# A second stage in three passes, its up projection by Strassen's seven products: decoder trunk on one Trainium2 core

## The chip, the cores and the metric

One core of a Trainium2 chip runs the whole kernel. The metric is the device time of one execution in microseconds. Engines go by the profile's names: PE multiplies matrices (PEld is its weight load), DVE, ACT and POOL work element by element, SP issues DMAs. PSUM has eight banks of 128 x 512 float32, in which PE leaves its sums.

## The reference

One layer of a decoder trunk, for 2048 prompt tokens and 32 sample tokens (8 sequences of 4) that share all weights, in float32:

```python
h = rms_norm(x, w_norm1) * (1 + sc1) + sh1
mix, ... = hybrid_mixer(h, ...)
x = x + gt1 * mix
h = rms_norm(x, w_norm2) * (1 + sc2) + sh2
x = x + gt2 * (jnp.square(jax.nn.relu(h @ w_up)) @ w_down)
y = rms_norm(x, w_norm_f)
```

The last step of the mixer is `concatenate([o_dn, o_gla]) @ w_o`. D is 1024; w_o is 1024 x 1024, w_up 1024 x 4096, w_down 4096 x 1024. The modulations sh, sc and gt come from a conditioning vector, one for the prompt and one for each sample sequence.

## The kernel before

Everything is kept transposed: features on the 128 partitions, tokens along the free dimension. There are 2080 tokens, the 32 samples first, in four groups (`TG`: 544, 512, 512, 512). Where a block is wider than PSUM's 512 it is cut (`BLK`: group 0 in two blocks of 272 columns, the others in one of 512). A float32 operand is split in two float32r parts, `hi` (a rounded copy) and `lo` (the rest), and `prod` (L239) makes a product of three matmuls for each 128 rows of the sum: hi x hi, hi x lo, lo x hi.

The first stage (`group`, L1132) goes group by group through the input projection and the two recurrences. It leaves the gated heads' two factors in DRAM (`oscr`, `zscr`).

The second stage (from L1230) runs in two halves, of groups 0 and 1, then 2 and 3. Each half has, for its two groups:

- `prep_o` (L1108): eight steps, each loads 128 rows of `oscr` and `zscr` on POOL's queue into `xo` and `zo` (two buffers each), multiplies them on DVE and splits the result (ACT the hi, DVE the lo).
- `out_proj` (L1253): eight products of 8 x 3 matmuls per block, `gated_add` (L1241) adds them to x on DVE, `sq_add` sums the squares.
- `norm2` (L1270): `sq_end` and `rsqrt` make the inverse root of the mean, then h is scaled, shifted and split into `hb` tiles.
- eight chunks (`ch`) of 512 hidden features: `up` (L1289) four times, with ReLU and Square on ACT and a split into the tiles `a` or `x`; then `down` (L1302) for eight output rows, with the sum over the chunks kept in SBUF by `gated_add`.
- `last_norm` (L1309) and the stores of y.

Weights come through `parts` (L205) and the six buffers `wb`. The first time, a weight of 128 x 1024 is loaded, ACT makes the hi (L225), another engine the lo (L226: DVE for the input projection, POOL for w_o, w_up and w_down), and both are stored in DRAM (`kept`, L201). Every later time both are loaded from there (L217). All weight DMAs are issued by SP in one order.

A tile framework lays the instructions out: it takes them in the order of the Python code, weighs what could run first, and writes for each engine a fixed sequence. An engine takes its own strictly in order. A tile's buffers go round; a new tile waits for the last reader of its buffer. Functions put into `late` are emitted at the next `flush()`.

## Time and profile before

| | us |
|---|---|
| median of 3 runs (lowest, highest) | 2911.71 (2907.19, 2912.94) |
| the profiled execution: its own time | 2916.36 |
| its span, first to last instruction | 2914.5 |
| PE busy / DVE busy / ACT busy / POOL busy | 2830.3 / 1488.0 / 889.3 / 265.6 |
| granted TensorE clock, mean | 0.987 |

The profile is one execution; its time lies 4.65 us above the median of the runs. Busy times are sums over the span. Matmuls overlap in the record: one of 512 columns is listed with some 0.40 us, and the next starts 0.23 us later, so rates are read from starts. The second stage's first matmul is at some 1212 us, its last at 2896.

### The profile page before, as it was taken

The numbers are of one execution on the slowest core, as the hardware profiler recorded it, in microseconds if no ns is written. First come the engines' busy times: TensorE is split into PE (matmuls) and PEld (weight loads), VectorE is DVE, ScalarE is ACT, GpSimd is POOL, SyncE is SP. The second block draws the span as 40 slices with busy tenths as digits, with TensorE's granted clock in tenths as the row PEclk, the third lists the DMA queues.
The fourth block names the chain that finished last, engine by engine and source line by source line (L and its number), as shares of the span: only waits on it lengthen the run. The fifth ranks groups of instructions, "written<-read, shape, count | busy, mean of one in ns | idle before, by whom it ended". The sixth has DMA issues, their size and how long they took to land.

```text
span 2914.5 us, 43962 instructions
## 1 busy us (share of the span) xinstructions
PE 2830.3 (97%) x17311; PEld 2395.6 (82%) x17311; DVE 1488.0 (51%) x3564; ACT 889.3 (31%) x2238; POOL 265.6 (9%) x204
## 2 busy tenths in 40 slices
PE   7999999999999999999999999999899999999997
PEld 5889977887778778888999999998788888888886
DVE  5997778666766776565233333334744222222225
ACT  3655534343444444323211221123222110011112
POOL 0100000000000100222221121122100000000000
PEclk9999999999999999999999999999999999999998
DMA  7565545456546445676333334334864222222224
GB/s 272 191 204 199 197 141 178 134 194 223 175 154 211 158 169 167 216 276 229 131 144 138 131 138 144 131 133 168 292 240 144 102 87 102 88 100 91 97 96 150
DMA packets 174272, 476.08 MB, mean 163 GB/s; under 512 B 36961, under 2 KB 50657, under 8 KB 173297
## 3 DMA queue, kind: packets, MB, share of 16 engines
q1 hardware_dynamic: 167520, 451.88, 44.5%
q0 software_dynamic: 6544, 21.38, 2.3%
q8 instruction: 137, 2.24, 0.3%
q14 instruction: 71, 0.57, 0.1%
HBM read 331.68 MB, written 141.79 MB: 162 GB/s over the span
## 4 chain that ended last, share of the span: by engine, by line
PE 81%; DVE 8%; DMA 5%; issue 3%; ACT 2%; POOL 1%; SPq 0%; DVEq 0%; POOLq 0%; ACTq 0%
PE gps L244 12%; PE gps L245 12%; PE gps L243 12%; PE cps L244 10%; PE cps L245 10%; PE cps L243 10%; PE gps L419 1%; PE mps L419 1%; DMA wb<-w_in 1%; DVE cv L837 1%; PE mps L1020 1%; DMA xo<-oscr 1%; PE mps L630 1%; PE cps L164 1%; DVE Um L915 1%
## 5 line engine op out<-in xcount | busy, mean ns | idle before, releaser
L243 PE MATMUL gps<-hb,wb 128*128 128x512 f32 (+1 forms) x1752 | 632.4, 361 | 5.9 <-ACT gkq L585 2.9
L245 PE MATMUL gps<-hb,wb 128*128 128x512 f32 (+1 forms) x1752 | 626.5, 358 | 2.4 <-POOL wb L226 1.7
L244 PE MATMUL gps<-hb,wb 128*128 128x512 f32 (+1 forms) x1752 | 627.3, 358 | 0.0
L243 PEld LDWEIGHTS gps<-hb,wb 128*128 128x128 f32 x1752 | 332.5, 190 | 59.5 <-issue 7.1
L245 PEld LDWEIGHTS gps<-hb,wb 128*128 128x128 f32 x1752 | 332.1, 190 | 45.8 <-POOL wb L226 1.9
L244 PEld LDWEIGHTS gps<-hb,wb 128*128 128x128 f32 x1752 | 332.3, 190 | 44.7 <-issue 2.7
L245 PE MATMUL cps<-hb,wb 128*128 128x512 f32 (+1 forms) x968 | 343.8, 355 | 4.8 <-POOL wb L226 4.8
L243 PE MATMUL cps<-hb,wb 128*128 128x512 f32 (+1 forms) x968 | 343.3, 355 | 4.9 <-DVE gas L1248 4.9
L244 PE MATMUL cps<-hb,wb 128*128 128x512 f32 (+1 forms) x968 | 343.8, 355 | 0.0
L226 POOL TENSOR_TENSOR wb<-wb 128x1024 fp32r<-128x1024 f32 x72 | 172.5, 2395 | 741.8 <-PE gps L244 408.6
L243 PEld LDWEIGHTS cps<-hb,wb 128*128 128x128 f32 x968 | 183.6, 190 | 32.1 <-issue 5.3
L245 PEld LDWEIGHTS cps<-hb,wb 128*128 128x128 f32 x968 | 183.6, 190 | 31.6 <-POOL wb L226 5.4
L244 PEld LDWEIGHTS cps<-hb,wb 128*128 128x128 f32 x968 | 183.5, 190 | 26.4 <-issue 0.2
L1296 ACT ACTIVATE e<-cps 128x512 f32<-128x512 f32 (+1 forms) x96 | 50.1, 522 | 499.2 <-PE cps L245 499.2
L225 ACT CAST wb<-wb 128x1024 fp32r<-128x1024 f32 (+1 forms) x104 | 109.3, 1051 | 295.2 <-DMA wb<-w_up 159.7
L1299 DVE CAST a<-e 128x272 fp32r<-128x272 f32 (+1 forms) x96 | 58.7, 613 | 251.9 <-ACT e L1297 251.8
L1299 DVE CAST x<-e 128x512 fp32r<-128x512 f32 x64 | 27.3, 427 | 277.6 <-ACT e L1297 277.6
L243 PE MATMUL cps<-a,wb 128*128 128x272 f32 (+1 forms) x460 | 149.5, 325 | 5.1 <-DVE gas L1248 3.7
L244 PE MATMUL cps<-a,wb 128*128 128x272 f32 (+1 forms) x460 | 149.4, 325 | 0.0
L245 PE MATMUL cps<-a,wb 128*128 128x272 f32 (+1 forms) x460 | 148.8, 324 | 0.0
L1296 ACT ACTIVATE e<-gps 128x512 f32<-128x512 f32 (+1 forms) x64 | 32.9, 514 | 341.7 <-PE gps L245 340.6
L1244 DVE SCALAR_TENSOR_TENSOR a<-cps,modT,a 128x512 f32<-128x512 f32 (+1 forms) x81 | 58.1, 717 | 134.5 <-PE cps L245 134.4
(472 smaller groups left out, 5199.6 us busy)
## 6 DMA issues: line engine op xcount, KB each, us to landing
wb<-k_w_in SPq DMA_DIRECT2D x168, 512.0 KB, 4.3
wb<-k_w_up SPq DMA_DIRECT2D x80, 512.0 KB, 4.2
wb<-k_w_down SPq DMA_DIRECT2D x80, 512.0 KB, 4.2
k_w_up<-wb SPq DMA_DIRECT2D x64, 512.0 KB, 2.8
k_w_down<-wb SPq DMA_DIRECT2D x64, 512.0 KB, 2.7
k_w_in<-wb SPq DMA_DIRECT2D x56, 512.0 KB, 3.4
wb<-k_w_o SPq DMA_DIRECT2D x48, 512.0 KB, 4.7
wb<-w_up SPq DMA_DIRECT2D x32, 512.0 KB, 3.6
```

Of the source, the lines that this page charges most:

```text
L164: T.matmul(ps[32 * j:32 * j + 32, :], lhsT=cs[:, 4 * hf + j, :], rhs=wt[hf][:, j, :], start=(hf == 0), stop=(hf == 1))
L225: S.copy(out=hi, in_=raw[:, 0:n])
L226: (V if name in ("w_in", "w_ts0", "w_ts1") else G).tensor_tensor(out=lo, in0=raw[:, 0:n], in1=hi.bitcast(F32), op=SUB)
L243: T.matmul(ps, lhsT=w[0][:, kw], rhs=x[0](kx), start=(i == 0), stop=False)
L244: T.matmul(ps, lhsT=w[0][:, kw], rhs=x[1](kx), start=False, stop=False)
L245: T.matmul(ps, lhsT=w[1][:, kw], rhs=x[0](kx), start=False, stop=(i == n - 1))
L419: T.matmul(ps, lhsT=h[hh][:, 4 * q + kk, c0:c0 + P], rhs=w[:, kk, :], start=(kk == 0 and i == 0), stop=(kk == 3 and i == 2))
L630: T.matmul(pa[0:i0, n, i0:i0 + 32], lhsT=ko[:, n, o:o + I, :], rhs=Q3[:, n, i0:i0 + 32], start=True, stop=True)
L837: V.scalar_tensor_tensor(out=cp, in0=raw[:, i:i + 512], scalar=wconv[:, ct, i:i + 1], in1=cp, op0=MUL, op1=ADD)
L1244: V.scalar_tensor_tensor(out=out[:, lo:c1], in0=ps[:, lo - c0:c1 - c0], scalar=modT[:, gv, 0:1], in1=x[:, lo:c1], op0=MUL, op1=ADD)
L1296: S.activation(out=r, in_=ps, func=AF.Relu)
L1299: V.tensor_copy(out=hi, in_=r)
```

## The change

The first stage keeps its code; its constants move into a pool of their own (`cm`) that is closed with it, so that the second stage has their space. The second stage is written anew:

- **Three passes** of two token halves take the place of two halves of two groups: 348 columns in each half of the first pass, 346 in the others (`NT`, `T0`). Every weight of the second stage is thus read three times, not twice.
- **Seven products for eight.** Two rows of 128 hidden features (f = 2j, 2j + 1) by two halves of the sum (k 0 to 3, 4 to 7) by two token halves are eight products of 4 x 3 matmuls. `up` makes them from seven, in Winograd's form of Strassen's scheme: products of sums of weights by sums of operands, then sums of products on DVE (`plus`), read from PSUM.
- **Made operands.** `norm_first` prepares the first token half's h and its split; `norm_second` prepares the second half's, and the four sums of both, each split in two. These seven pairs stay in SBUF for the pass (`hb`, `e0`, `e1`). `up_weights` loads two rows of w_up in the first pass, makes four sums on DVE, splits all seven and stores them in DRAM (`kept_up`); the later passes load these.
- **Order.** In passes two and three the last down projection of the previous pass's second half (`before`) stands after the out projection, ahead of the up projection. The first half's last down projection carries `prep_o` of the next pass's first half.
- The lo of every weight is made on DVE; POOL has no arithmetic in the second stage but three scalings at its end.

```diff
@@ parts
-        (V if name in ("w_in", "w_ts0", "w_ts1") else G).tensor_tensor(out=lo, in0=raw[:, 0:n], in1=hi.bitcast(F32), op=SUB)
+        V.tensor_tensor(out=lo, in0=raw[:, 0:n], in1=hi.bitcast(F32), op=SUB)
...
+    NT = [348, 346, 346]
+    T0 = [0, 696, 1388]
...
+    def prod4(ps, w, x):
+        for k in range(4):
+            T.matmul(ps, lhsT=w[0][:, k], rhs=x[0][:, k], start=(k == 0), stop=False)
+            T.matmul(ps, lhsT=w[0][:, k], rhs=x[1][:, k], start=False, stop=False)
+            T.matmul(ps, lhsT=w[1][:, k], rhs=x[0][:, k], start=False, stop=(k == 3))
...
+    def norm_second(p, acc, x, b1, b2, h0, rest):
+        n = NT[p]
+        rb = inv_rms(acc, n)
...
+        def two(o, k, v):
+            S.copy(out=o[0][:, k], in_=v)
+            V.tensor_tensor(out=o[1][:, k], in0=v, in1=o[0][:, k].bitcast(F32), op=SUB)
+
+        def value(v, k):
+            V.scalar_tensor_tensor(out=v, in0=x[:, k], scalar=a2[:, k, 0:1], in1=rb, op0=MUL, op1=MUL)
+            S.activation(out=v, in_=v, func=AF.Identity, bias=modT[:, 24 + k, 0:1])
+            return v
+
+        top, low = [], []
+        for k in range(4):
+            top.append(value(fill(("xo", "zo")[k % 2], 2, n), k))
+            low.append(value(fill("s", 4, n), 4 + k))
+            V.tensor_tensor(out=h0[:, k], in0=top[k], in1=h0[:, k], op=SUB)
+            t = fill("xr", 2, n)
+            V.tensor_tensor(out=t, in0=low[k], in1=h0[:, k], op=SUB)
+            two(o_t2, k, t)
+            V.tensor_tensor(out=h0[:, 4 + k], in0=h0[:, 4 + k], in1=t, op=SUB)
+            two(o_t1, k, h0[:, k])
+        for k in range(4):
+            V.tensor_tensor(out=top[k], in0=low[k], in1=top[k], op=SUB)
+            two(o_t3, k, top[k])
+        for k in range(4):
+            two(o_b, k, low[k])
+        for k in range(4):
+            two(o_t4, k, h0[:, 4 + k])
+        return [b1, b2, o_t2, o_t1, o_t3, o_b, o_t4]
+
+    def up_weights(p, j):
...
+        if p:
+            for i in range(7):
+                store_parts()
+                w = tile2()
+                Y.dma_start(out=w.bitcast(F32), in_=kept_up[j, i])
+                yield views(w)
+            return
...
+        make = {2: ((s1, a21, a22, ADD), (s2, s1, a11, SUB)), 4: ((s3, a11, a21, SUB),), 5: ((s4, a12, s2, SUB),)}
+        for i, x in enumerate((a11, a12, s2, s1, s3, s4, a22)):
+            for out, u, v, op in make.get(i, ()):
+                V.tensor_tensor(out=out, in0=u, in1=v, op=op)
+            store_parts()
+            w = tile2()
+            S.copy(out=w[:, 0:512], in_=x)
+            V.tensor_tensor(out=w[:, 512:1024], in0=x, in1=w[:, 0:512].bitcast(F32), op=SUB)
+            stores.append((kept_up[j, i], w.bitcast(F32)))
+            yield views(w)
+
+    def up(p, j, b, ah):
...
+        def finish(x, i, f):
+            S.activation(out=x, in_=x, func=AF.Relu)
+            S.activation(out=x, in_=x, func=AF.Square)
+            S.copy(out=ah[i][:, f], in_=x)
+            V.tensor_tensor(out=ah[i][:, 4 + f], in0=x, in1=ah[i][:, f].bitcast(F32), op=SUB)
...
+        s, v = fill("s", 4, n), fill("s", 4, n)
+        S.copy(out=s, in_=product(0))
+        finish(plus(fill("e", 3, n), s, product(1)), 0, f0)
+        plus(s, s, product(2))
+        plus(v, s, product(3))
+        ps = product(4)
+        plus(s, s, ps)
+        finish(plus(fill("e", 3, n), v, ps), 1, f0 + 1)
+        finish(plus(v, v, product(5)), 1, f0)
+        finish(plus(s, s, product(6)), 0, f0 + 1)
...
+    for p in range(3):
...
+        prep_o(p, 1, o[1], ("xo", "zo"))
...
+        acc = out_proj(p, 0, o[0], x[0])
+        first = []
+        late.append(lambda: first.extend(norm_first(p, acc, x[0])))
...
+        acc1 = out_proj(p, 1, o[1], x[1])
+        ops = []
+        late.append(lambda: ops.extend(norm_second(p, acc1, x[1], *first)))
+        if before:
+            before()
+        else:
+            flush()
+        for ch in range(8):
+            ah = [space(t, n, F32R) for t in AU[p]]
+            for j in range(2):
+                up(p, ch * 2 + j, ops, ah)
+                flush()
...
+        if p < 2:
+            ab = half_tiles()
+            between = lambda k: prep_o(p + 1, 0, o_first(p + 1, ab), ("xo", "zo"), [k])
+        down_last(p, 0, ah[0], x[0], between)
+        before = lambda p=p, ah=ah, x=x: down_last(p, 1, ah[1], x[1])
+    before()
```

The built programs show where this stands on the engines. First DVE at the end of the stage's first out projection. Before, the second normalization of group 1 (L1275 scales, L1287 makes the lo) stands between instructions that split group 0's up products (L1299, L1300); L282 and L271 to L273 are the chain of the mean:

```order
L282 TENSOR_SCALAR cv<-mps 128x512
L1300 TENSOR_TENSOR a_14660<-e,a_14658 128x272
L271 SCALAR_TENSOR_TENSOR cv<-cv 128x512
L272 TENSOR_TENSOR cv<-cv 128x512
L273 SCALAR_TENSOR_TENSOR cv<-cv 128x512
L1275 SCALAR_TENSOR_TENSOR xr<-x_13688,a_121,cv 128x512 x2
L1299 CAST a_14658<-e 128x272
L1287 SCALAR_TENSOR_TENSOR hb<-xr,modT,hb 128x512 x2
L1275 SCALAR_TENSOR_TENSOR xr<-x_13689,a_121,cv 128x512 x2
L1300 TENSOR_TENSOR a_14660<-e,a_14658 128x272
```

In the changed program the chain (L1281, L273 to L275) is followed by `norm_second` (L1349 scales, L1346 makes a lo, the others make sums); L1400 makes the lo of a weight of the up projection. Here its beginning:

```order
L1281 TENSOR_SCALAR cv<-mps 128x348
L273 SCALAR_TENSOR_TENSOR cv<-cv 128x348
L274 TENSOR_TENSOR cv<-cv 128x348
L1400 TENSOR_TENSOR wb<-wr,wb 128x512
L275 SCALAR_TENSOR_TENSOR cv<-cv 128x348
L1349 SCALAR_TENSOR_TENSOR xo<-u_14080,a_124,cv 128x348
L1349 SCALAR_TENSOR_TENSOR s<-u_14080,a_124,cv 128x348
L1349 SCALAR_TENSOR_TENSOR zo<-u_14080,a_124,cv 128x348
L1357 TENSOR_TENSOR u_14127<-xo,u_14127 128x348
L1349 SCALAR_TENSOR_TENSOR s<-u_14080,a_124,cv 128x348
L1359 TENSOR_TENSOR xr<-s,u_14127 128x348
```

and its end, up to the first products' sums (L1416) and the first high row's split (L1413); L1396 makes a sum of weights:

```order
L1346 TENSOR_TENSOR hb<-zo,e_14449 128x348
L1346 TENSOR_TENSOR hb<-s,e_14450 128x348 x4
L1346 TENSOR_TENSOR hb<-u_14127,hb 128x348 x4
L1416 TENSOR_TENSOR e<-s,cps 128x348
L1400 TENSOR_TENSOR wb<-wr,wb 128x512
L1416 TENSOR_TENSOR s<-s,mps 128x348
L1396 TENSOR_TENSOR wr<-wr 128x512
L1413 TENSOR_TENSOR u_14535<-e,u_14535 128x348
L1416 TENSOR_TENSOR s<-s,cps 128x348
L1396 TENSOR_TENSOR wr<-wr 128x512
L1416 TENSOR_TENSOR s<-s,gps 128x348
L1416 TENSOR_TENSOR e<-s,gps 128x348
```

What moved: no instruction that takes an up product out of PSUM stands between the chain and the last made operand any more; 44 instructions of `norm_second` stand there in one piece.

Second ACT, while weights are made for the first time. Before, a weight's cast (L225) stands between the ReLU (L1296) and the Square (L1297) of a block:

```order
L1296 ACTIVATE e_15646<-cps_15621 128x272
L225 CAST wb_15813<-wb_15809 128x1024
L1297 ACTIVATE e_15646<-e_15646 128x272
L1296 ACTIVATE e_15676<-gps_15651 128x272
L1297 ACTIVATE e_15676<-e_15676 128x272
L1296 ACTIVATE e_15706<-cps_15681 128x512
L1297 ACTIVATE e_15706<-e_15706 128x512
L1296 ACTIVATE e_15744<-gps_15719 128x272
L225 CAST wb_15911<-wb_15907 128x1024
```

In the change, at the end of a chunk's up projection in the first pass, casts of the down projection's weights (L227) stand ahead of the last ReLUs (L1410), Squares (L1411) and casts (L1412):

```order
L227 CAST wb_16045<-wb_16042 128x1024
L1410 ACTIVATE e_15991<-e_15991 128x348
L1411 ACTIVATE e_15991<-e_15991 128x348
L1412 CAST u3_15726<-e_15991 128x348
L1410 ACTIVATE s_15886<-s_15886 128x348
L1411 ACTIVATE s_15886<-s_15886 128x348
L1412 CAST u3_15726<-s_15886 128x348
L227 CAST wb_16115<-wb_16111 128x1024
L1410 ACTIVATE s_15885<-s_15885 128x348
L1411 ACTIVATE s_15885<-s_15885 128x348
L1412 CAST u2_15725<-s_15885 128x348
```

What moved: the last row of the up projection (s_15885) now stands on ACT behind the cast of the down projection's second weight (wb_16115), and so behind that weight's load.

## Rows read from the trace of the kernel before

**Rows 1.** The page: busy time, share of the span and instructions of each engine.

```profile
PE 2830.3 (97%) x17311; PEld 2395.6 (82%) x17311; DVE 1488.0 (51%) x3564; ACT 889.3 (31%) x2238; POOL 265.6 (9%) x204
```

**Rows 2.** Stretches of 100 us, with their columns: first half, second half.

```profile
core 0: us, PE busy (x) PEld busy (x) DVE busy (x) ACT busy (x) POOL busy (x), PEclk, DMA share, GB/s
...
1400.00:1500.00 100.00, 100.00 (x625) 90.90 (x624) 32.51 (x73) 20.61 (x33) 19.63 (x9) 1.00 0.39 140
...
2300.00:2400.00 100.00, 100.00 (x433) 80.76 (x432) 22.92 (x36) 12.34 (x20) 0.00 (x0) 1.00 0.27 95
```

**Rows 3.** Timeline of PE: first starts of three runs of matmuls.

```profile
1999.79 0.28 PE L243 MATMUL cps<-hb,wb 128*128 128x272 f32 x1
...
2005.80 0.40 PE L243 MATMUL gps<-hb,wb 128*128 128x512 f32 x1
...
2011.38 0.28 PE L243 MATMUL cps<-hb,wb 128*128 128x272 f32 x1
```

**Rows 4.** Stretches where PE waits, one of heavy traffic, the end; columns as above.

```profile
1220.00:1280.00 60.00, 48.61 (x346) 47.40 (x344) 29.35 (x56) 14.86 (x21) 30.84 (x37) 0.91 0.87 300
2030.00:2070.00 40.00, 27.41 (x158) 24.84 (x157) 27.93 (x55) 12.08 (x19) 13.84 (x19) 0.87 0.78 262
2110.00:2120.00 10.00, 9.82 (x43) 7.65 (x42) 3.89 (x6) 1.90 (x3) 1.61 (x3) 1.00 0.96 365
2896.50:2914.50 18.00, 0.96 (x4) 0.30 (x2) 10.51 (x20) 2.08 (x5) 5.10 (x6) 0.58 0.35 117
```

**Rows 5.** Timeline of SP's queue: loads of the out and up projections' weights.

```profile
1207.66 0.33 SPq L221 DMA_DIRECT2D wb<-w_o  x1
...
1221.16 0.38 SPq L221 DMA_DIRECT2D wb<-w_o  x1
...
1274.15 35.75 SPq L217 DMA_DIRECT2D wb<-k_w_o  x16
```

**Rows 6.** Timeline of DVE at the end: last eviction, first scaling.

```profile
2894.61 0.48 DVE L1244 SCALAR_TENSOR_TENSOR a<-gps,modT,a 128x256 f32<-128x256 f32 x1
...
2899.74 3.47 DVE L1317 SCALAR_TENSOR_TENSOR a<-a,w_norms,xr 128x256 f32<-128x256 f32 x5
```

**Rows 7.** DVE's groups of the second stage: lo parts, evictions; busy time, mean.

```profile
L1300 DVE TENSOR_TENSOR x<-e,x 128x512 fp32r<-128x512 f32 x64 | 44.3, 692 | 2.1
...
L1300 DVE TENSOR_TENSOR a<-e,a 128x272 fp32r<-128x272 f32 x64 | 28.2, 442 | 2.0
L1244 DVE SCALAR_TENSOR_TENSOR x<-cps,modT,x 128x512 f32<-128x512 f32 x37 | 27.7, 750 | 73.0 <-PE cps L245 73.0
...
L1244 DVE SCALAR_TENSOR_TENSOR x<-cps,modT,x 128x272 f32<-128x272 f32 x38 | 19.0, 499 | 20.3 <-PE cps L245 20.3
```

**Rows 8.** Line L226, the low part of a weight, on POOL and DVE; ns min/median/max.

```profile
L226 POOL TENSOR_TENSOR wb<-wb x72: 2347/2398/2497, 1201.1 to 2044.0; 128x1024 fp32r<-128x1024 f32 x72
...
L226 DVE TENSOR_TENSOR wb<-wb x32: 1205/1218/1292, 26.1 to 318.9; 128x1024 fp32r<-128x1024 f32 x28, 128x1056 fp32r<-128x1056 f32 x2, 128x1088 fp32r<-128x1088 f32 x2
```

**Rows 9.** Timeline of DVE between the halves.

```profile
2054.24 0.69 DVE L1118 TENSOR_TENSOR xo<-xo,zo 128x512 f32<-128x512 f32 x1 [3.98 <-DMA xo<-oscr]
...
2055.23 0.71 DVE L265 TENSOR_TENSOR cv<-cv,ce 128x544 f32<-128x544 f32 x1
2055.86 0.18 DVE L1248 TENSOR_TENSOR gas<-cps,modT 128x32 f32<-128x32 f32 x1
2055.96 0.68 DVE L1120 TENSOR_TENSOR hb<-xo,hb 128x512 fp32r<-128x512 f32 x1
2056.56 0.18 DVE L1250 TENSOR_TENSOR x<-x,gas 128x32 f32<-128x32 f32 x1
...
2070.85 0.69 DVE L1118 TENSOR_TENSOR xo<-xo,zo 128x512 f32<-128x512 f32 x1 [0.80 <-DMA xo<-oscr]
```

**Rows 10.** The page's DMA issues: KB each, median us from issue to landing.

```profile
wb<-w_up SPq DMA_DIRECT2D x32, 512.0 KB, 3.6
```

More of the change, by code (lines that the diff above doesn't have):

```diff
@@ L1172, in mix @@
             elif hd == 1:
-                hl = [hp.tile([P, 8, 544], F32R, name="hb") for _ in range(2)]
+                hl = half_tiles() if g == NG - 1 else [hp.tile([P, 8, 544], F32R, name="hb") for _ in range(2)]
                 if g < NG - 1:
@@ L1250, in gated_add, with sq_one, inv_rms @@
             V.tensor_tensor(out=out[:, 0:32], in0=x[:, 0:32], in1=t, op=ADD)
-    def out_proj(g, oh, ol, xk):
-        tg = TG[g]
-        acc = sp.tile([P, 544], F32, name="cv")
+    def sq_one(acc, k, x, n):
+        if k == 0:
+            S.activation(out=acc, in_=x, func=AF.Square)
+        else:
+            e = fill("ce", 1, n)
+            S.activation(out=e, in_=x, func=AF.Square)
+            V.tensor_tensor(out=acc, in0=acc, in1=e, op=ADD)
+    def inv_rms(acc, n):
+        rb = fill("cv", 4, n)
+        ps = mps()[:, 0:n]
+        T.matmul(ps, lhsT=ones, rhs=acc, start=True, stop=True)
+        V.tensor_scalar(out=acc, in0=ps, scalar1=1.0 / D, scalar2=EPS, op0=MUL, op1=ADD)
+        rsqrt(rb, acc)
+        return rb
@@ L1258, in out_proj @@
[L1258 to L1262 removed]
+            xr = fill("xr", 2, n)
+            G.dma_start(out=xr, in_=a["xA"][k, :, T0[p] + i * n:T0[p] + i * n + n])
+            ps = bps(n)
+            prod(ps, w, o, range(8), range(8))
@@ L1302, in down @@
[L1302 to L1310 removed]
+            S.activation(out=h[:, off:], in_=t[:, off:], func=AF.Identity, bias=modT[:, 24 + k, 0:1])
@@ new lines, in up, with plus, product @@
+    def up(p, j, b, ah):
+        n = NT[p]
+        f0 = 2 * (j % 2)
+        def finish(x, i, f):
[3 more added lines that the diff above has]
+            V.tensor_tensor(out=ah[i][:, 4 + f], in0=x, in1=ah[i][:, f].bitcast(F32), op=SUB)
+        def plus(out, x, ps):
+            V.tensor_tensor(out=out, in0=x, in1=ps, op=ADD)
+            return out
+        w = up_weights(p, j)
+        def product(i):
+            turn[0] += 1
+            ps = (gps, mps, cps, mps, cps, gps, mps, cps)[turn[0] % 8]()[:, 0:n]
+            prod4(ps, next(w), b[i])
+            return ps
+        s, v = fill("s", 4, n), fill("s", 4, n)
[8 more added lines that the diff above has]
+        finish(plus(s, s, product(6)), 0, f0 + 1)
+        for _ in w:
+            pass
@@ new lines, in down, with down_last @@
+    def down(w, n, ah, dd, k, x, off):
+        ps = bps(n)
+        prod(ps, w, (lambda f: ah[:, f], lambda f: ah[:, 4 + f]), range(dd * 4, dd * 4 + 4), range(4))
+        gated_add(x[:, k], ps, 40 + k, x[:, k], off)
+    def down_last(p, i, ah, x, between=None):
+        n = NT[p]
+        acc = fill("cv", 4, n)
+        for dq in range(4):
+            w = split("w_down", (7, dq))
+            for dd in range(2):
+                k = dq * 2 + dd
+                down(w, n, ah, dd, k, x, 32 if p == 0 and i == 0 else 0)
+                if k == 0:
+                    flush()
+                sq_one(acc, k, x[:, k], n)
+                if between:
+                    between(k)
+        late.append(lambda: last_norm(p, i, acc, x))
```

234 lines of the change are left out of this document (108 added, 126 removed).

## The prediction

> **What bounds the kernel now.** Read the busy shares first: PE is busy 97% of the span and DVE 51% [rows 1]. A busy PE alone says little, so look next at the stretches by 100 us. In the second stage PE is busy without a break, at 625 matmuls in 100 us in the first half (blocks of 272, 272 and 512 columns) and 433 in the second (512 only), and DVE has 23% to 33% of work there [rows 2]. So the time of the second stage is its number of matmuls by what each takes, plus the few places where PE waits. For what each takes, read starts, not durations: 48 matmuls of 272 columns start in the 6.01 us between the first two rows of [rows 3], 125.2 ns each, and the next 24 of 512 columns take 5.58 us, 232.5 ns each; the second half's 433 in 100 us make 231 ns. PE waits in two places: at the start of the stage (48.6 of 60 us busy, at a granted clock of 0.91, while the DMA moves 300 GB/s) and between the halves (27.4 of 40 us busy) [rows 4]; and it has nothing to do in the last 18 us, the last normalization [rows 4].
>
> **1. Matmuls.** Before: five token blocks, each with 64 + 256 + 256 products of three matmuls, 8640 in all: 3456 of 272 columns and 5184 of 512 (96 of these cut in two). 3456 x 0.1252 + 5184 x 0.2313 = 432.7 + 1199.1 = 1631.8 us. After: the out and down projections have six blocks, 6 x 320 x 3 = 5760; the up projection has 3 passes x 16 pairs x 7 products x 12 = 4032. Of these 9792, 3264 have 348 columns and 6528 have 346. Between the two measured widths a column costs 106.1 / 240 = 0.442 ns, so 348 columns take 125.2 + 33.6 = 158.8 ns and 346 take 157.9: 518.3 + 1030.8 = 1549.1 us. The term is **-83 us**; 1 ns more or less per matmul is 10 us, and both ends are kept.
> By the Trainium skill (TensorE: Matmul & The Clock Gate, Back-to-back issue gap) an isolated matmul takes N / 2.4 + 2.5 ns. The trace does not agree, with 125 and 231 ns where this gives 116 and 216. By the page the term would be 80 us.
>
> **2. Out projection of the first pass.** Its loads hold the stage's start. Before, 1.57 MB of weight (load and two stores), 0.28 of x and 0.52 of the next block's heads go with each of eight steps; after, 1.57, 0.18 and 0.36. Three weights are loaded by 1220 us [rows 5]; five loads, six pairs of stores and all else come later: 8.9 + 8 x 0.80 = 15.3 MB before, 8.9 + 8 x 0.54 = 13.2 after. At the 300 GB/s of [rows 4] that is 7 us less, while the matmuls of that block take 384 x 0.1252 - 192 x 0.1588 = 17.6 us less. So 10.6 us of term 1 are not had: **+11**. Low end +3 (the DMA at the 365 GB/s of [rows 4]), high end +18 (nothing of the wait shrinks).
>
> **3. The second half's operands, first pass.** Before, the second normalization runs beside the up projection of the other block, as the order on DVE shows; now the third to the seventh product of every pair need operands of both halves, and nothing stands between. After the last out product come the chain of the mean (5.1 us from the last product's eviction to the first scaling in [rows 6]) and 44 DVE instructions of 348 columns. One such takes 0.44 to 0.69 us at 272 and 512 columns, 0.52 between them [rows 7], and the next one starts after 0.60 at 512 [rows 9], so 0.45 to 0.52 here: 20 to 23 us. The last operand is there at 27 us, the pair ends at 29, where seven products need 13.4, and the next pair's third weight stands behind 14 more DVE instructions: **+17**. Low end +10 (0.45 each, and the next pair's first two products go ahead), high end +24 (0.52 and a cast's wait in every second step).
>
> **4. The same in passes two and three.** There the previous pass's last 96 down matmuls (15.2 us) and two products (3.8) stand between. DVE has 28 of the 44 instructions and 16 of that down projection ahead of the third and fourth product: 5.1 + (28 + 16) x 0.48 = 26 us against 19; so 7 each, **+14**. Low end 0, high end +24.
>
> **5. Between the passes.** Two boundaries in place of one. The one cost 12.6 us of idle PE and some 2.4 of granted clock 0.87 [rows 4], and what PE waits for is the stream of head loads: two buffers each, one step in 3.3 us over the five from 2054.24 to 2070.85 [rows 9]. Now eight steps stand under 96 matmuls (15.2 us) and part of the first out product (3.3): with two steps loaded ahead, six at 3.3 are 20 us, 1.5 more. Bytes: 8 weights of 0.52 MB and 16 head loads of 0.18 under these 96, 16 weights, 24 loads of heads and x and 8 outputs under the next 192, 21.1 MB under 45.5 us of PE, of which 3.1 lie ready in the six weight buffers. At 365 GB/s that is 4 us too long, at 300 it is 15. I take 9 each, nearer to the mixed stretch than the best one: 18 - 15 = **+3**. Ends: 2 x 3 - 15 = -9 and 2 x 18 - 15 = +21.
> The Trainium skill (DMA: Bandwidth & Descriptors, Specifications) states some 358 GB/s from HBM for a core. The trace shows 365 over 10 us, and 300 where stores are mixed in. By the page a boundary would lose some 5 us, an estimate.
>
> **6. Weights made on DVE in the first pass.** The low parts leave POOL, and sums are added. Each pair costs DVE seven low parts and four sums of 512 columns and eleven instructions of 348 on products: 11 x 0.69 + 7 x 0.58 + 4 x 0.52 = 13.7 us by durations, 11 x 0.60 + 11 x 0.45 = 11.6 by starts [rows 7, 9], against 13.3 us of PE. That is tight, but eleven of a chunk's 22 of the 512s lie under the down projection, where DVE has 16 x 0.58 + 4 x 1.22 and small ones, 17 of 30.5 us, and eight PSUM buffers let PE run ahead. On ACT the down projection's first high parts now stand among the last products' ReLUs, as the order shows, and the second waits for a load that finds a free buffer some two products before the end and lands after 3.6 us or more [rows 10]: up to 1 us in each of eight chunks, **+6**. Low end 0, high end +24 (3 us each). Its stores cost nothing while the DMA keeps up: 2 x 9 + 4 x 3 transfers of 0.52 MB per chunk of 57 us are 274 GB/s. What POOL loses (72 subtractions of 2.4 us; DVE takes 1.22 [rows 8]) no one waits for but at the start.
>
> **7. The end.** One block of 346 columns in place of two of 256: eight scalings, three of them on POOL, after one chain. **-2**, between -6 and +3. Nothing changes in the first stage, whose instructions stand as they did up to its last 100 us.
>
> **Sum.** -83 + 11 + 17 + 14 + 3 + 6 - 2 = -34 us on the profiled execution's own 2916.36. That one lies 4.65 above the median of the three runs, 2911.71, so I forecast 2878 for the median. All low ends give -85 and with term 1's -95, all high ends +31.
>
> **Rivals.** *The stalls are covered.* DVE's instructions overlap more than their starts show and the boundary loads are early: terms 2 to 5 at or near their low ends, -83 + 3 + 10 + 0 - 9 + 3 - 2 = -78, 2834 us. Against it: the order on DVE leaves nothing between. 12%.
> *DVE becomes the bound of the first pass.* If a pair takes 15.3 us there (13.7 by durations and 1.6 of waits on ACT), 16 pairs lose 32 us in place of 6: 2904. For it: 13.7 against 13.3. Against it: the work under the down projection. 17%.
> *The weight stream falls behind, and it is slower than before.* In passes two and three each product needs its own 0.52 MB; a product is 1.90 us. The 16 loads from 1274.15 us took 2.23 us each [rows 5]. If that is what the queue gives, 224 products lose 0.33 each, 74 us: 2952. It decides from 1.90 us per load, 276 GB/s. Against it: those loads waited for buffers, and 365 GB/s were reached [rows 4]. 8%.
> That the change does not do what it says is out: the built order has the 9792 matmuls.
>
> **How the numbers follow.** The forecast has 63%. A measurement of this kernel can tell 0.2% from no change, so the bounds are 2905.9 and 2917.5. Of the forecast's 63, 60 lie below and 2 within; of the 17 some 10 below and 4 within; the 12 below; the 8 above. Faster 0.82, same 0.06, slower 0.12. The range for 8 in 10 leaves out the third rival and the lowest part of the first: 2840 to 2914.
>
> **What would show it.** Matmuls of 348 columns start every 159 ns in pass one's down projection, else term 1 is wrong. PE is idle some 15 to 20 us after the first pass's out projection, waiting for DVE's operands, and 15 to 16 us around each later boundary and its operands together. In the first pass's chunks PE is busy 98% or more; in the two others 100%, with DMA at some 275 GB/s in the up projection. PE waits for weight loads there, or gaps in every pair of the first pass, would make the prediction wrong.

## The result and the profile after

| | before | changed |
|---|---|---|
| median of 4 runs, us (lowest, highest) | 2910.21 (2907.19, 2912.94) | 2936.11 (2935.12, 2944.14) |
| ratio to before, 95% interval | | 1.0095 [1.0074, 1.0116] |
| the profiled execution: its own time, its span | 2916.36, 2914.5 | 2936.26, 2934.4 |

The change makes the kernel 26 us slower where 34 us faster was forecast, outside the range of 2840 to 2914. A ratio is not taken from the two medians and can differ a little from theirs. In what follows "x us less than the changed kernel" is a difference of two such ratios times 2911; with intervals of some 0.002 on each, under 8 us is not told from nothing.

The page's first row answers to [rows 1]: PE has 43 us less to do, in a longer span.

```profile
PE 2787.7 (95%) x18369; PEld 2561.3 (87%) x18369; DVE 1759.0 (60%) x4226; ACT 1088.6 (37%) x2765; POOL 116.9 (4%) x177
```

Two stretches of 100 us (columns as in [rows 2]), of the first pass's chunks and of the second's:

```profile
1400.00:1500.00 100.00, 97.69 (x610) 96.77 (x609) 67.36 (x138) 37.12 (x66) 0.00 (x0) 1.00 0.73 260
2000.00:2100.00 100.00, 100.00 (x628) 99.54 (x628) 35.55 (x68) 25.07 (x52) 0.00 (x0) 1.00 0.63 211
```

628 matmuls in 100 us are 159.2 ns each. Inside the chunks of passes two and three PE never waits, and in the first pass it loses little. So the loss must be at the start of the stage and between the passes. Take three stretches of the changed kernel: the start of the stage (from its first matmul to the end of the first up projection) and its two boundaries between passes (from the last down projection of one pass to the end of the next pass's first chunk). Behind them stands the boundary between the halves of the kernel before:

```profile
1203.30:1346.90 143.60, 110.52 (x580) 102.57 (x579) 92.27 (x216) 59.92 (x127) 21.48 (x40) 0.87 0.70 247
...
1755.90:1949.40 193.50, 164.12 (x947) 157.93 (x946) 113.83 (x243) 61.73 (x134) 24.64 (x46) 0.93 0.76 264
2320.70:2515.80 195.10, 166.78 (x947) 161.68 (x946) 107.67 (x222) 59.40 (x130) 20.36 (x38) 0.91 0.69 239
```

```profile
2023.00:2270.20 247.20, 234.43 (x1068) 192.07 (x1067) 132.16 (x209) 57.25 (x90) 28.71 (x43) 0.98 0.63 220
```

A changed boundary holds 936 products (the rest of the 947 are sums for the mean): 149.0 us at 159.2 ns. So 44.5 and 46.1 us are lost. The stage's start has 552 products (87.9 us) and 22 of the first stage (5 us): 50.7 lost. With the prices of the prediction the same sum over the kernel before gives 23.2 at its boundary and 21.5 at its start. The whole stage by places, in us:

| | before | changed | growth | forecast |
|---|---|---|---|---|
| matmuls at their rate | 1631.8 | 1558.9 | -73 | -83 (term 1) |
| lost at the stage's start | 21.5 | 50.7 | +29 | +28 (2, 3) |
| lost in the first pass's other chunks | 0.7 | 7.6 | +7 | +6 (6) |
| lost at boundaries | 23.2 | 90.6 | **+67** | +17 (4, 5) |
| lost elsewhere | 3.6 | 2.2 | -1 | 0 |
| end | 18.5 | 15.5 | -3 | -2 (7) |

With a first stage that ended some 7 us earlier in this execution the growth is +19, and the spans differ by 19.9. Of the 54 us between the forecast's -34 and this, 50 are one row, the boundaries; the matmuls' 10 and the first stage's 7 nearly cancel.

What PE waits for there, in all of the second boundary (engine, operation, releaser: us in total, times, longest):

```profile
PE mps L1280 <- DVE cv L1275: 10.7, 2, 6.9
PE cps L247 <- DMA wb<-k_w_o: 6.3, 2, 5.7
PE gps L245 <- ACT u L1412: 3.8, 1, 3.8
PE mps L1288 <- DMA wb<-k_up: 3.3, 1, 3.3
```

These four are 24 of the 46 us, and smaller gaps make another 10. Nearly all of the rest is the clock. Stretches of 5 us around one wait, after the second out projection:

```profile
2420.00:2425.00 5.00, 3.61 (x23) 3.31 (x21) 2.05 (x4) 0.99 (x2) 0.54 (x1) 1.00 0.97 328
2425.00:2430.00 5.00, 0.00 (x0) 0.00 (x0) 0.80 (x3) 0.49 (x1) 0.00 (x0) 0.64 0.34 133
2430.00:2435.00 5.00, 4.50 (x14) 4.02 (x15) 1.97 (x4) 1.26 (x3) 0.00 (x0) 0.50 0.00 0
2435.00:2440.00 5.00, 5.00 (x29) 5.00 (x28) 4.45 (x10) 2.46 (x6) 0.00 (x0) 0.84 0.60 210
2440.00:2445.00 5.00, 5.00 (x33) 5.00 (x33) 5.00 (x12) 4.03 (x10) 0.00 (x0) 1.00 0.70 236
```

PE stands 7 us, and then runs 14 matmuls in 5 us at a granted clock of 0.50, the lower of its two levels (1.2 of 2.4 GHz), before 33 again. By the starts of the matmuls, some 65 in the first boundary and 80 in the second came at the slow distance (0.29 us and not 0.16): 8 and 10 us that no row of waits lists.

The largest wait is for a mean (L1280 needs the sum of L1275): 6.9 us for that of the second half, 3.8 for that of the first. PE's last out product ends at 2421.5, so why is its sum late by 7? POOL's timeline, with the loads of the rows of x for the second out projection, and DVE's at the end of it:

```profile
2388.46 0.54 POOL L1299 DMA_DIRECT2D xr<-xA  x1 [1.09 <-DVE u L1262]
2404.98 1.07 POOL L1299 DMA_DIRECT2D xr<-xA  x2 [15.99 <-ACT u L1329]
2409.96 1.07 POOL L1299 DMA_DIRECT2D xr<-xA  x2 [3.90 <-DVE u L1262]
2416.66 0.54 POOL L1299 DMA_DIRECT2D xr<-xA  x1 [5.63 <-DVE u L1262]
2417.77 0.54 POOL L1299 DMA_DIRECT2D xr<-xA  x1 [0.57 <-DVE u L1262]
2422.09 0.54 POOL L1299 DMA_DIRECT2D xr<-xA  x1 [3.78 <-DVE u L1262]
```

```profile
2428.73 0.58 DVE L1262 SCALAR_TENSOR_TENSOR u<-gps,modT,xr 128x346 f32<-128x346 f32 x1 [3.58 <-DMA xr<-xA]
2429.92 0.52 DVE L1275 TENSOR_TENSOR cv<-cv,ce 128x346 f32<-128x346 f32 x1 [0.62 <-ACT ce L1274]
```

The eviction of the last product adds its row of x, and that row was asked for only at 2422.09. POOL's loads stood 16 us until the first normalization (L1329) had let go of `xr`: the rows of x and that normalization's temporary share two buffers. Then the rows come by ones and twos. The list of DMA issues gives what one takes from issue to landing (KB, us):

```profile
xr<-xA POOLq DMA_DIRECT2D x32, 173.0 KB, 5.3
```

The Trainium skill (DMA: Bandwidth & Descriptors, Anatomy of one DMA) fits some 2.0 us plus bytes / 436e3 for a transfer by this path, 2.4 us for such a row, an estimate; the 5.3 us of this trace, under load, decide.

The change did not bring this sharing. In the kernel before, `norm2` takes `xr` too (L1274), and POOL stood even longer for it, but PE did not wait for that mean. Its loads there, and the stretch of its two out projections and the first up projection:

```profile
2156.86 1.20 POOL L1258 DMA_DIRECT2D xr<-xT  x2 [25.92 <-DVE hb L1287]
```

```profile
2088.70:2225.60 136.90, 136.72 (x584) 109.06 (x584) 68.22 (x103) 34.68 (x55) 8.04 (x15) 1.00 0.65 232
```

There the second out projection lasts 45 us and 24 matmuls of 512 columns (5.5 us) stand between it and its mean. In the change it lasts 31 us, with 12 matmuls of 346 (1.9 us) behind it. So it seems that the change took away the time in which the rows caught up; that is read from the two traces and not tried.

### The profile page after: what moved, and what is told of

Same layout as the page of the kernel before. It is cut to its first block, busy times and chain, and to the rows that moved or that the text cites. A ratio compares the mean times of both kernels' runs of the same rounds, so it can differ in the third digit from the quotient of the medians.

```text
span 2934.4 us, 48244 instructions
## 1 busy us (share of the span) xinstructions
PE 2787.7 (95%) x18369; PEld 2561.3 (87%) x18369; DVE 1759.0 (60%) x4226; ACT 1088.6 (37%) x2765; POOL 116.9 (4%) x177
## 5 line engine op out<-in xcount | busy, mean ns | idle before, releaser
L247 PE MATMUL gps<-hb,wb 128*128 128x512 f32 (+3 forms) x1272 | 455.4, 358 | 17.9 <-DVE wb L228 9.0
L245 PE MATMUL gps<-hb,wb 128*128 128x512 f32 (+3 forms) x1272 | 460.2, 362 | 8.4 <-ACT gkq L587 2.9
L246 PE MATMUL gps<-hb,wb 128*128 128x512 f32 (+3 forms) x1200 | 431.7, 360 | 0.0
L245 PE MATMUL cps<-u,wb 128*128 128x346 f32 (+1 forms) x928 | 302.6, 326 | 9.7 <-ACT u L1412 7.0
L247 PE MATMUL cps<-u,wb 128*128 128x346 f32 (+1 forms) x928 | 298.5, 323 | 1.3 <-DMA wb<-k_w_down 1.3
L246 PE MATMUL cps<-u,wb 128*128 128x346 f32 (+1 forms) x928 | 299.5, 324 | 0.1
L245 PEld LDWEIGHTS gps<-hb,wb 128*128 128x128 f32 x1272 | 242.9, 191 | 45.1 <-issue 7.3
L247 PEld LDWEIGHTS gps<-hb,wb 128*128 128x128 f32 x1272 | 242.3, 191 | 45.7 <-DVE wb L228 9.8
L246 PEld LDWEIGHTS gps<-hb,wb 128*128 128x128 f32 x1200 | 229.1, 191 | 27.5 <-issue 2.0
L1262 DVE SCALAR_TENSOR_TENSOR u<-cps,modT,u 128x346 f32<-128x346 f32 (+2 forms) x232 | 132.3, 572 | 194.6 <-PE cps L247 192.9
L245 PE MATMUL gps<-u,wb 128*128 128x346 f32 (+1 forms) x608 | 198.6, 327 | 4.4 <-ACT u L1412 3.8
L247 PE MATMUL gps<-u,wb 128*128 128x346 f32 (+1 forms) x608 | 197.3, 324 | 4.3 <-DVE wb L228 3.6
L246 PE MATMUL gps<-u,wb 128*128 128x346 f32 (+1 forms) x608 | 197.1, 324 | 0.0
L245 PEld LDWEIGHTS cps<-u,wb 128*128 128x128 f32 x928 | 176.1, 190 | 14.3 <-ACT u L1412 10.8
L246 PEld LDWEIGHTS cps<-u,wb 128*128 128x128 f32 x928 | 176.6, 190 | 1.5 <-DVE u L1413 0.6
L1262 DVE SCALAR_TENSOR_TENSOR u<-gps,modT,u 128x346 f32<-128x346 f32 (+2 forms) x152 | 87.1, 573 | 151.4 <-PE gps L247 151.2
L247 PEld LDWEIGHTS cps<-u,wb 128*128 128x128 f32 x928 | 176.3, 190 | 1.6 <-DMA wb<-k_w_down 1.6
L1289 PE MATMUL mps<-hb,wb 128*128 128x346 f32 (+1 forms) x504 | 164.6, 327 | 1.1 <-DVE hb L1346 1.1
L1289 PE MATMUL cps<-hb,wb 128*128 128x346 f32 (+1 forms) x504 | 162.5, 322 | 0.5 <-DVE hb L1346 0.4
L1410 ACT ACTIVATE e<-e 128x346 f32<-128x346 f32 (+1 forms) x96 | 47.6, 495 | 228.1 <-DVE e L1416 228.0
L1288 PE MATMUL cps<-hb,wb 128*128 128x346 f32 (+1 forms) x360 | 117.1, 325 | 5.9 <-ACT hb L1345 5.4
L245 PEld LDWEIGHTS gps<-u,wb 128*128 128x128 f32 x608 | 115.6, 190 | 6.8 <-ACT u L1412 5.4
```

The lines of the kernel that those rows point to most:

```text
L245: T.matmul(ps, lhsT=w[0][:, kw], rhs=x[0](kx), start=(i == 0), stop=False)
L246: T.matmul(ps, lhsT=w[0][:, kw], rhs=x[1](kx), start=False, stop=False)
L247: T.matmul(ps, lhsT=w[1][:, kw], rhs=x[0](kx), start=False, stop=(i == n - 1))
L1262: V.scalar_tensor_tensor(out=out[:, off:], in0=ps[:, off:], scalar=modT[:, gv, 0:1], in1=x[:, off:], op0=MUL, op1=ADD)
L1288: T.matmul(ps, lhsT=w[0][:, k], rhs=x[0][:, k], start=(k == 0), stop=False)
L1289: T.matmul(ps, lhsT=w[0][:, k], rhs=x[1][:, k], start=False, stop=False)
```

## Experiments

**Which part costs: the three passes or the seven products.**

`eight_products`: up in the old way, in the new passes.

```diff
-            prod4(ps, next(w), b[i])
+            prod(ps, w, xs, range(8), range(8))   # 2 rows x 2 halves
```

> Three passes as in the change, but the up projection with its eight products: no sums of weights or operands, weights of the up projection stored as hi and lo, each used for both token halves. 576 matmuls more, 91 us at 158 ns. Theory S (the stalls belong to the made operands): the first chunk's loss of 27 us, the 8.2 and 6.9 us at the second up projections' start and the 9 us of the first pass's chunks go; 2936 + 91 - 45 = 2982. Theory T (they belong to the three passes and their loads): only some 15 us go, 3012.

Measured 2974.51, ratio 1.0231 [1.0208, 1.0254]: 40 us more than the changed kernel, nearer to theory S. Yet of the boundaries' 90 us 69 are still there (38.0 and 31.2), and 37.5 of the start's 50.7. So the seven products win 40 of their 91 us, and three passes with eight products are 67 us slower than the kernel before.

**Order of queues, and the place of one product.** The first theory was a chain across queues. SP's own timeline speaks for it, with stores of y between loads of w_o:

```profile
2333.96 22.69 SPq L219 DMA_DIRECT2D wb<-k_w_o  x9
2363.28 0.83 SPq L1471 DMA_DIRECT2D o_y<-u  x2
2364.20 0.41 SPq L219 DMA_DIRECT2D wb<-k_w_o  x1
2364.72 7.84 SPq L1471 DMA_DIRECT2D o_y<-u  x6
2372.65 38.14 SPq L219 DMA_DIRECT2D wb<-k_w_o  x22
```

`y_on_pool`, `y_late` and `ones_later`:

```diff
-            Y.dma_start(out=a["o_y"][k, :, T0[p]
+            (Y if p == 2 else G).dma_start(out=a["o_y"][k, :, T0[p]
```
```diff
-            if k == 0:
+            if k == 0 and (p == 0 or i == 1):
                 flush()
```
```diff
# down_last
-                if k == 0:
+                if k == 2:
                     flush()
```

> The stores of y of the first two passes are issued by POOL in place of SP; nothing else is edited. Theory A (a chain of queues): between the passes the loads of w_o stand on SP behind the stores of y, these wait for DVE's scalings, and these stand on DVE behind products of heads that wait for their loads. Then PE's waits for w_o there (8.2 us at 1800, 5.7 at 2365) go, with the low clock behind them: 12 to 25 us less than the 2936 of the change, and the out projections of passes two and three lose under 8 us each in place of 15 and 19. Theory B (traffic): the DMA has more to move between the passes than it can in the time; then the order of the queue is worth under 5 us.

Measured 2938.71, ratio 1.0107 [1.0081, 1.0134]: nothing won. PE's waits in the second boundary, to be held against the four above:

```profile
PE mps L1280 <- DVE cv L1275: 14.5, 3, 5.7
...
PE cps L247 <- DMA wb<-k_w_o: 0.6, 1, 0.6
```

The wait for w_o did go, from 6.3 to 0.6 us, and the wait for the mean grew from 10.7 to 14.5. The two out projections of a pass lost 15.0 and 18.9 us together, as in the changed kernel; the loss moved from the first one to the second.

> The last normalization of the previous pass's first half, and so its stores of y, is emitted one out projection later (with the first normalization of the new pass). Theory A: in the third pass, where 25 loads of w_o now stand ahead of the first store, the out projection loses under 8 us in place of 19; some 8 to 20 us less than 2936 in all. Theory B: within 5 us of 2936.

Measured 2934.97, ratio 1.0089 [1.0067, 1.0112]: no gain that can be told; the second boundary lost 38.8 in place of 46.1, the first 47.4 in place of 44.5. Theory A had under 8 us for the third pass's out projections; they lost 18.7.

> The product by which the second normalization of passes two and three gets its mean stands 36 matmuls, not 12, into the down projection. Theory A2: PE waits there (4.0 us at 1862, 6.9 at 2426) only because that product stands too early; the 24 matmuls (3.8 us) then run in the wait: 6 to 12 us less than 2936, with the low clock that follows each wait. Theory B2: DVE's 44 instructions set when the up projection goes on; the wait then moves behind the first two up products, and the time stays within 3 us of 2936.

Measured 2936.62, ratio 1.0095 [1.0066, 1.0124]. As theory B2 says; the waits moved.

**Bytes or buffers.** `w_o_half`, `one_head_factor`, `three_buffers`, `w_o_reused`:

```diff
# w_o_half, passes two and three
-            for i in range(2):
+            for i in range(1 if name == "w_o" and len(passes) > 1 else 2):
...
-            return w
+            return w[0], w[-1]
```
```diff
# one_head_factor
-            q.dma_start(out=z, in_=zscr[k, :, c:c + n])
+            if not p: q.dma_start(out=z, in_=zscr[k, :, c:c + n])   # else z = o
```
```diff
# three_buffers; the scaled rows of norm_second, in the same names, get three too
-            o = sp.tile([P, 348], F32, name=tags[0])
+            o = sp.tile([P, 348], F32, name=tags[0], bufs=3)        # z too
```
```diff
# w_o_reused
-        for k in range(8):
-            w = split("w_o", k)
+        for m, k in enumerate((5, 6, 7, 4, 3, 2, 1, 0) if i else range(8)):
+            w = held[k - 5] if k > 4 else split("w_o", k)
```

> In passes two and three only the hi of w_o is loaded and stands in for the lo too: half of w_o's bytes are left out (4.2 MB in each half of a pass), no matmul. Theory B (traffic): from 2321 to 2389 us the changed kernel moves some 19.5 MB at 278 GB/s under 45.5 us of matmuls; 15.3 MB take 55 us, so the last down and the first out projection lose 10 us in place of 28 and 25: 2936 - 33 = 2903. Theory C (the heads' two buffers on POOL's queue set the pace, whatever else is loaded): they still lose 20 or more each, 2925 or above.

Measured 2911.91, ratio 1.0002 [0.9989, 1.0015]: 27 us less than the changed kernel, near theory B's 33.

> In passes two and three the second factor of the heads isn't loaded, the first is multiplied by itself: 2.8 MB and 16 loads on POOL's queue less between two passes. Theory B: 16.7 MB at 278 GB/s are 60 us, 14.5 lost each in place of 28 and 25, so 24 us less: 2912, and less is won than by the half of w_o. Theory C: half of the heads' stream goes, 36 to 50 us less, 2886 to 2900, and more is won than by w_o.

Measured 2937.3, ratio 1.0088 [1.0068, 1.0108]: nothing, where both theories had 24 us or more.

> Three buffers in place of two for each of the heads' two factors. Theory C: the loads start earlier, 10 to 25 us less than 2936. Theory B: the same bytes in the same time, within 5 us of 2936.

Measured 2916.8, ratio 1.0039 [1.0019, 1.0059]: 16 us less, as theory C says, with not a byte less. The profiled execution, its fastest, gains 10 us at the stage's start and 13 at the boundaries.

> The second out projection of each pass begins with the three weights that the first one ended with, still in the six buffers, and goes back down from there: 3 of 8 weights of w_o are not loaded again, 3.1 MB less in each pass, no other byte, matmul or buffer changed. Theory B (bytes): 11 us of DMA time at 278 GB/s less in each pass; the losses of the out projections (29, 15, 19 us) and of what follows fall by 10 to 20 us in all: 2916 to 2926. Theory C (the depth of the small streams of heads and x): within 5 us of 2936.

Measured 2935.08, ratio 1.0081 [1.0056, 1.0105]: 4 us, not told from none. (Each out projection loads w_o anew, so w_o is read six times in the stage, not three.) So fewer bytes alone won nothing in two of three runs, and a deeper stream won without fewer bytes. `w_o_half` does not decide between them: a weight that takes one buffer of six and not two also lets loads go out earlier.

**The made operands.** `few_made` and `lo_on_pool`:

```diff
-            two(o_t2, k, t)
...
-            two(o_t4, k, h0[:, 4 + k])
-        return [b1, b2, o_t2, o_t1, o_t3, o_b, o_t4]
+            two(o_t1, k, value(fill(("xo", "zo")[k % 2], 2, n), k))
+            two(o_b, k, value(fill("s", 4, n), 4 + k))
+        return [b1, b2, o_b, o_t1, o_t1, o_b, o_b]
```
```diff
-            two(o_b, k, low[k])
+            two(o_b, k, low[k], G)        # and o_t4: lo by POOL
```

> The second normalization makes only the second half's scaled rows and their split (16 DVE instructions of 44); no difference or sum of operands is made, and five products read these in place of the made ones. Left out: 28 DVE instructions and 12 copies on ACT in each pass, no matmul. Theory D (DVE's made operands): the first chunk's up projection loses 27 - 28 x 0.48 = 14 us in the first pass and 1 to 2 in place of 8.2 and 6.9 in the others: some 27 us less, 2909. Rival (the weights' loads after the wait of the norm set the start in passes two and three): only the first pass wins, 13 us, 2923.

Measured 2913.03, ratio 0.9999 [0.9983, 1.0015]: 28 us less. The stage's start, to be held against 143.6 us in the first of the stretches above:

```profile
1201.40:1335.30 133.90, 105.96 (x581) 101.47 (x580) 79.34 (x187) 52.58 (x110) 21.43 (x40) 0.89 0.76 268
```

The first chunk's up projection loses 14.7 there in place of 27, as forecast to 1 us, and those of the second and third pass lose 0.6 each in place of 8.9 and 8.5. So DVE's made operands do cost what terms 3 and 4 say they cost there; the rival, by which only the first pass wins, is out.

> Eight of the 28 lo parts of the second normalization (the pairs of the last two products) are made on POOL, which has nothing else there, in place of DVE. Theory D: DVE has 36 instructions in place of 44 between the mean and the first sums, 3.8 us less in each pass: 8 to 12 us less than 2936. Rival: a POOL subtraction (2.4 us for 1024 columns, so some 0.8 for 346) is late for its product or slows DVE; within 4 us.

Measured 2953.55, ratio 1.0135 [1.0120, 1.0151]: 12 us more, and the first up projections of passes two and three lose 12.2 and 12.9 us in place of 8.9 and 8.5. POOL's groups show the likely reason:

```profile
L1346 POOL TENSOR_TENSOR hb<-s,e 128x346 fp32r<-128x346 f32 x8 | 12.9, 1617 | 36.9 <-ACT e L1345 36.9
L1346 POOL TENSOR_TENSOR hb<-u,hb 128x346 fp32r<-128x346 f32 x8 | 11.1, 1400 | 2.3 <-ACT hb L1345 2.3
```

One takes 1.4 to 1.6 us there where 0.8 was worked out from the 2.4 us of 1024 columns [rows 8], and eight of them take some 12 us, where DVE was to save 3.8.

**The rows of x.** `x_rows_free` gives the first normalization another tile for its temporary:

```diff
-            t = fill("xr", 2, n)
+            t = fill("e", 3, n)
             h = h0[:, k]
```

> The first normalization's temporary row comes from another tile (e) and no longer from the two buffers into which the rows of x are loaded. In the changed kernel the loads of x for the second out projection stand 23.7, 17.0 and 16.0 us on POOL until that normalization is done; the eight rows then come by twos, 5 to 7 us apart, and the mean of the second half is late. Theory X: PE's waits for that mean (7.5, 4.0, 6.9 us) fall to some 3 us or less each, with their low clock: 10 to 18 us less than 2936. Rival (the chain of the mean and the weights' loads set it): within 4 us.

Measured 2912.17, ratio 1.0014 [0.9997, 1.0031]: 24 us less by one name, more than theory X has. POOL's first loads for the second out projection, and PE's wait for the mean in the second boundary:

```profile
2392.29 1.06 POOL L1299 DMA_DIRECT2D xr<-xA  x2 [10.05 <-DVE u L1262]
```

```profile
PE mps L1280 <- DVE cv L1275: 3.2, 1, 3.2
```

The loads wait for the eviction ahead of them and no longer for L1329, and the wait for the mean falls from 10.7 to 3.2 us. What follows the out projections in the second boundary loses 12.4 us in place of 21.6. Of the whole gain 13 us are at the two boundaries and 11 at the stage's start.

**Together.**

> The three edits of this series and three buffers for the heads together. If the waits they remove are different ones, the gains add: 19 (measured) + 14 + 10 + 15 = 58 us less than 2936, 2878, clearly below the 2910 of the kernel before. If they are one wait seen four times, it stays at the best single one: some 2915.

Measured 2921.88, ratio 1.0033 [1.0022, 1.0044]. It holds `three_buffers`, `x_rows_free`, `lo_on_pool` and `w_o_reused`. Neither number comes out, and it is no faster than `x_rows_free` alone; `lo_on_pool`, which costs by itself, is the likely reason. So the two edits that had helped and leave nothing out were put together without it (`x_free_three_buffers`), and the heads of passes two and three were loaded into `wr`, four steps deep (`x_free_heads_in_wr`), then with `y_late` (`x_free_wr_y_late`).

```diff
+            if p:
+                t = mp.tile([P, 1024], F32, name="wr", bufs=4)
+                o, z = t[:, 0:n], t[:, 512:512 + n]
```

> The edits of x_rows_free and three_buffers together. Theory X and C (two different small streams, each with too few buffers, make PE wait between the passes): the gains add, 24 + 19 = 43 us less than 2936: 2893. Rival (both free the same wait): 2910.

Measured 2905.95, ratio 0.9984 [0.9966, 1.0003]: 32 us less than the changed kernel, between the two numbers and nearer to the rival's. Three buffers, 16 us alone, win 9 on top of `x_rows_free`: in part the two free the same wait.

> As x_rows_free, and from the second pass on the heads' two factors are loaded into the four tiles wr, which only the first pass uses: four steps deep in place of two, and two head loads more can be under way before the previous pass ends. Theory C: the out projections of passes two and three lose under 8 us each in place of 15 and 19: 2912 - 20 = 2892. Rival (what is left there is the order on SP, stores of y ahead of loads of w_o): within 5 us of 2912.

Measured 2919.76, ratio 1.0012 [0.9998, 1.0025]: as `x_rows_free`; the rival is right. The out projections lost 16.3 and 9.3, the down projections ahead of them 16.6 and 8.3, more than the 11.7 and 5.1 without it.

> As x_free_heads_in_wr, and the last normalization of the previous pass's first half one out projection later, as in y_late. If the order on SP holds the loads of w_o once the small streams are mended, 5 to 15 us less than x_free_heads_in_wr; if not, within 5 us of it.

Measured 2908.03, ratio 0.9982 [0.9965, 1.0000]: 9 us less than `x_free_heads_in_wr`. The order on SP, where no gain could be told at first, is worth something now.

> The eight products of eight_products (2974.5) with the edits of x_rows_free and three_buffers. If the waits that these remove come from the three passes, it wins what the changed kernel wins, some 40 us: 2935, and the seven products are worth some 40 us as before. If they come from the made operands, it wins under 15: 2960 or above.

Measured 2956.43, ratio 1.0145 [1.0122, 1.0168]: 25 us won, between the two theories. With the streams mended the seven products are worth 47 us (1.0145 against 0.9984), before that 40; with some 9 us of noise on each, the two are not told apart.

> x_free_three_buffers (2906) with y_late. With the small streams mended, the loads of w_o between the passes wait on SP behind the stores of y; x_free_wr_y_late lost 9.5 and 7.1 us in its out projections where x_free_heads_in_wr lost 16.8 and 9.8. Theory A, in second place: 5 to 12 us less, 2894 to 2901, below the kernel before by more than the interval. Rival: within 4 us of 2906.

Measured 2896.54 (7 runs), ratio **0.9939 [0.9918, 0.9961]**: 45 us less than the changed kernel and 0.6% faster than the kernel before. Its two boundaries and PE's largest waits in the second:

```profile
1740.30:1923.00 182.70, 163.30 (x946) 158.92 (x946) 111.56 (x241) 61.13 (x132) 24.36 (x46) 0.93 0.79 279
2294.30:2471.20 176.90, 162.44 (x945) 158.53 (x945) 105.42 (x220) 59.14 (x129) 18.26 (x34) 0.94 0.74 261
```

```profile
PE mps L1288 <- DMA wb<-k_up: 3.4, 1, 3.4
PE gps L245 <- ACT u L1412: 3.1, 1, 3.1
PE gps L247 <- DMA wb<-k_w_o: 3.0, 2, 2.6
```

The gain is 13 us over `x_free_three_buffers`. The wait for the mean is gone from the top, and the boundaries lose 33.7 and 27.9 us in place of 44.5 and 46.1.

> The same, and the low part of w_o made on POOL again, as in the kernel before. PE waits 13.4 us for these low parts on DVE in the first pass of x_free_three_buffers. If they are late because DVE has other work, 5 to 10 us less than x_free_three_y_late; if the raw weights' loads set them, none; if POOL's 2.4 us for each hold up its own loads of x, up to 8 us more.

```diff
-        V.tensor_tensor(out=lo, in0=raw[:, 0:n], in1=hi.bitcast(F32), op=SUB)
+        (G if name == "w_o" else V).tensor_tensor(out=lo, in0=raw[:, 0:n], in1=hi.bitcast(F32), op=SUB)
```

Measured 2910.0, ratio 0.9992 [0.9974, 1.0009]: 15 us more, where the last of the three cases had up to 8. The first pass's two out projections lose 35 us in place of 20. In this mended kernel, at least, the low parts of w_o stand better on DVE.

## Why the prediction was wrong

**The step that failed is the sum of terms 4 and 5, the boundaries: +17 forecast, +67 measured.** With the 15 us that the prediction found at the one boundary before, term 5 priced 18 us lost at both boundaries up to the end of the out projections, and term 4 priced 14 behind them. Measured by the starts of the matmuls, in us, both boundaries together, one execution of each kernel:

| | priced | changed | `x_rows_free` | `few_made` | `x_free_three_y_late` |
|---|---|---|---|---|---|
| last down projection of the first half, two out projections | 18 (5) | 52.0 | 51.3 | 55.9 | 36.6 |
| last down projection of the second half | 14 (4), with the next row | 16.9 | 3.9 | 12.4 | 1.5 |
| the next pass's first chunk | | 21.5 | 22.3 | 4.6 | 23.6 |

- Term 4 let the chain of the mean start at "the last product's eviction", taken right behind the product. The eviction needs a row of x, and these rows come through two buffers that the first normalization holds, so that POOL stands 16 to 17 us for them at the boundaries. `x_rows_free` shows it: the second row falls by 13 us, a quarter of the miss of 50. The rest of its 24 us is at the stage's start, outside this miss. What term 4 did price, DVE's instructions, was right in kind and near in size: `few_made` takes 17 us off the third row.
- Term 5 lost 52.0 us for 18. It priced "the stream of head loads". In the kernel before, PE's largest wait at the boundary was already one for a mean, on DVE:

```profile
PE mps L281 <- DVE cv L265: 4.5, 1, 4.5
```

- Depth and order of the small streams and of the stores, mended together in `x_free_three_y_late`, take 15 us off the first row. That the heads' own buffers were too few is not shown: three of them won 16 us alone and 9 on top of `x_rows_free`, four steps in `wr` won none.
- 36.6 us are left in the first row, twice what term 5 has, and their cause stays open. The bytes are a likely one. The same stretches, from the last down projection to the end of the second out projection, first of the changed and then of the mended kernel:

```profile
1755.90:1859.90 104.00, 85.14 (x486) 81.63 (x485) 56.95 (x125) 31.81 (x66) 20.37 (x38) 0.92 0.88 306
2320.70:2421.50 100.80, 85.57 (x486) 83.10 (x485) 51.31 (x105) 28.43 (x61) 19.82 (x37) 0.92 0.82 284
```

```profile
1740.30:1839.70 99.40, 86.84 (x486) 84.44 (x486) 55.72 (x124) 31.55 (x65) 19.55 (x37) 0.91 0.91 319
2294.30:2384.30 90.00, 83.38 (x486) 81.45 (x486) 50.98 (x106) 29.12 (x62) 18.26 (x34) 0.94 0.90 318
```

  The bytes are the same in both, some 32 and 29 MB, for 76 us of matmuls each; the mended kernel moves them at 319 and 318 GB/s. An estimate: at the 365 GB/s of [rows 4] they take 87 and 78 us. Term 5 set its bytes against the first 45.5 us alone, and so left out that the second out projection has 16 weights of its own to load. The runs with fewer bytes were made while the other waits still stood. Not all of it is loads, though. In the first of the two mended stretches PE also waits for low parts that DVE makes (L228) of the last weights of the first pass, which no term has there:

```profile
PE cps L247 <- DMA wb<-k_w_o: 7.0, 2, 3.7
PE cps L247 <- DVE wb L228: 2.8, 1, 2.8
PE gps L247 <- DVE wb L228: 1.5, 1, 1.5
```

- For the new boundaries only idle time was priced. 8 and 10 us per boundary are matmuls at the slow clock, and 12 at the start. In the mended kernel's boundaries PE idles some 41 us in place of 69, but the slow clock costs 19 us there as in the changed kernel.

**Term 1** was right in kind: 159.2 ns per matmul where 157.9 to 158.8 was worked out between two widths, -73 us in place of -83, at the dear end of its 10 us.

**Terms 2 and 3** come out in their sum, +29 for +28, and that is luck. The first pass's out projections grew by 5 us (from 19 to 24) where term 2 has 11, and its first up projection by 25 (from 2 to 27) where term 3 has 17, just past its high end. The mechanism of term 3 holds: `few_made` took from the first chunk what DVE's 28 instructions had been priced at. But the late mean is in it too: `x_rows_free` took 11 us off this place, 8 of them off the up projection.

**Term 6** holds: +7 for +6. **Term 7** holds: 15.5 us at the end for 18.5.

**The rivals.** The faster one, by which the stalls are covered, did not come: they are larger than forecast. The slower rival was the weights' stream in passes two and three. It did not come: 211 GB/s and no wait in the second stretch of 100 us above. Nor did DVE bound the first pass: PE is busy 97.7% there. The change is slower by a mechanism that no rival had, though both its parts (two buffers, one order on POOL) could be read from the program.

Left open: how much of `w_o_half`'s 27 us is bytes, and how much the earlier loads; the two were not tried apart. Nor were fewer bytes tried in the mended kernel, nor its edits in the kernel before, so its 0.6% is not the worth of the change alone.

## What to carry to other kernels

When work is cut into more passes, price the seams by the start and the landing of each small stream: how many buffers it has, who else uses their name, and when the first load of it can be issued. Bytes over rate is only the lower bound. A hold that cost nothing before can cost once the work that hid it is shorter. Where several waits stand at one seam, taking one away alone can show little until others are mended: `y_late` alone won 2 us, not told from none, and 13 us with the streams mended (some 9 us of noise on each, so that it won more is likely, not shown). And PE's waits can cost the slow clock behind them as well: 8 to 12 us at each of these three places.
